# A hybrid decoder trunk in exact-split fp32r: one in-place weight sum per early seven-product group becomes an accumulating load

## The chip, the cores and the metric

The kernel runs on one core of one Trainium2 chip. The metric is device time in microseconds (us) of one execution. A core has a matrix engine (PE, with its weight loads as PEld), a vector engine (DVE), a scalar engine (ACT), a general engine (POOL, GpSimd), and SP, which here only issues transfers. Each engine runs its own instructions strictly in order; engines wait for one another and for transfers by semaphores. Transfers are issued from SP's queue, and some from POOL's.

## The reference, cut to what matters

One decoder layer takes 528 prompt tokens (16 of them meta tokens) and 8 sample tokens, width 2048:

```
h = rmsnorm(x) @ w_in                       # 2048 x 8704: q, k, v, z_a, u, z_s, g_a, g_s
o = sliding-window attention with sinks(q, k, v)
y = S5 state-space branch(u)                # diagonal complex recurrence per group
br_a = (o * silu(z_a)) @ w_attn_out ; br_s = (y * silu(z_s)) @ w_ssm_out
out = x + (sigmoid(g_a) * br_a + sigmoid(g_s) * br_s) @ w_out
```

The result is wanted in fp32. Nearly all the time goes to the products with the weights.

## The kernel before, in words

**Split products.** A weight unit is 128 partitions x 1024 fp32 elements (512 KB). For use it is split in two: ACT casts it to a high part `whi` (L1074), DVE makes the low part `wlo = raw - whi` (L1075), and PE forms high times high, high times low and low times high for each of eight 128x128 pieces, 24 matmuls of 260 columns per product of a seven-product group.

**Seven products in place of eight.** The class `Quads` (L1026 to L1086) serves places where a 2x2 block product is made with seven products (Strassen's way) in place of eight. A group has four units, loaded as `raw[0]` to `raw[3]`, and seven products, numbered here 0 to 6 in the order in which `make` splits their weights. Product 0 uses unit 0 and product 1 unit 1. Before product 2 DVE adds unit 2 into unit 1, in place; before product 3 it adds unit 0 into unit 1 (tuple `(1, 0)` in `SUMS`) and unit 0 into unit 2 (tuple `(2, 0)`); before product 4 it adds unit 3 into unit 1. Product 5 uses unit 3, and product 6 uses unit 2 as summed. So the sum (2, 0) is wanted by product 6 only. These sums are L1073.

There are 15 **early groups** (two column blocks of `w_in` each; `self.fourth` is None there) and, at the kernel's end, 8 **late groups** for `w_out`. In the first late group (`r < 7 and self.fourth`) the sum (2, 0) is already made without DVE: POOL issues a second load of unit 0 whose transfer adds into `raw[2]` (L1070). In all others DVE makes it.

**Order.** Loads, casts, sums and splits are written some three products ahead of the matmuls and carry high priority. A scheduler then sets, before the program runs, the order of the instructions on each engine. The accumulator banks of PE are emptied by ACT (`keep3`, L1394; L1416) and DVE (L1422, L1417, L1432, then the evacuation L1200). In an early group PE's order is: product 0, then product 6 of the group before in the midst of it, 1, 2, 3, a few matmuls of 5, then 4, then the rest of 5. Product 4 adds into the bank that product 2 filled, and so may start only when ACT's L1394 has emptied that bank.

**Work beside it.** During the early groups POOL computes the constants of the state-space branch (`ssm_prep`, L149 to L299, on `OnPool`): some 200 small instructions, one chain, each waiting for one before it, tile `work`. Its result is stored by L1499 (`kept`) and transposed by PE (L291) later.

Of the kernel before, what the change touches and what calls it, by code (L numbers as in the profile page):

```python
# [12 lines left out]
ALU = mybir.AluOpType  # L13
# [976 lines left out]
class Stream:  # L990
# [20 lines left out]
    def make(self, i):  # L1011
        with self.tc.high_priority(offset=HIGH):
            self.piece(i, self.tiles(i), slice(0, 8))
# [12 lines left out]
class Quads:  # L1026
# [29 lines left out]
    def make(self, r):  # L1056
        nc = self.nc
        q, s = divmod(r, 7)
        if self.LOADS[s] is not None:
            self.load(4 * q + self.LOADS[s] + 4)  # L1060
        if r < 7 and self.fourth:
            s = (0, 1, 2, 5, 3, 4, 6)[s]
        t = self.raw[4 * q + self.SRC[s]]
        pool, bufs = (self.pool, 3) if r % (3 + self.mp) < 3 else (self.more, self.mp)
        hi = pool.tile([P, 8, P], F32R, name="whi", bufs=bufs)
        lo = pool.tile([P, 8, P], F32R, name="wlo", bufs=bufs)
        with self.tc.high_priority(offset=HIGH):
            for oi in self.SUMS[s]:
                if r < 7 and self.fourth and oi == (2, 0):
                    nc.gpsimd.dma_start(out=self.raw[2], in_=self.w[self.first], accum_op=ALU.add)  # L1070
                    continue
                o, i = (self.raw[4 * q + j] for j in oi)
                nc.vector.tensor_tensor(out=o, in0=o, in1=i, op=ALU.add)  # L1073
            nc.scalar.copy(out=hi, in_=t)  # L1074
            nc.vector.tensor_tensor(out=lo, in0=t, in1=hi.bitcast(F32), op=ALU.subtract)  # L1075
        self.parts[r] = hi, lo
# [873 lines left out]
```

## Time and profile before

| | |
|---|---|
| three runs, median | 1264.08 us (1263.49 to 1266.17) |
| span of the profiled execution | 1262.3 us; the page gives no other time for it. The median run is 1.8 us above this span |
| PE busy | 1250.9 us, 99% |
| DVE busy / ACT / POOL | 980.6 / 628.7 / 266.1 us |
| early groups | from about 112 to 420 us of the span |
| POOL's constants | from 112.8 to 266 us |
| late groups | from about 1096 us to the end |

Times in rows of the profile are microseconds from the span's start; a mean or a minimum of one instruction is in ns where the view says so. A row of the time line has start, duration, engine, line, operation, tiles and, in brackets, the idle time ahead and what ended it; "x3" merges three like instructions that follow each other. A row of the busy time by stretch has the length of the stretch, then busy time and number of instructions of PE, PEld, DVE, ACT and POOL, the granted clock of PE, the share of the transfer engines and GB/s. A busy PE means back-to-back matmuls, about 0.12 us apart.

### The profile page before, as it was taken

To read this page: it belongs to the slowest core of one execution; us is meant where nothing else is said; L and a number is where in the kernel's file an instruction comes from. 1 tells how busy PE (TensorE), PEld (TensorE's weight loads), DVE (VectorE), ACT (ScalarE), POOL (GpSimd) and SP (SyncE) were. 2 spreads that over 40 slices of the span, in tenths; PEclk is the share of its full clock that TensorE was granted. 3 is DMA by queue.
4 is the path that set the end of the run, shared out by engine and by line. 5 is a ranking of instruction groups with operands and counts; after the bars stand their busy time and mean duration, and the time that the engine had idled before them with its cause. 6 is when DMAs were issued, how large, how long until landed. Compare 5 with 4: busy or idle time off the path is not lost.

```text
span 1262.3 us, 26537 instructions
## 1 busy us (share of the span) xinstructions
PE 1250.9 (99%) x10357; PEld 1227.7 (97%) x10357; DVE 980.6 (78%) x1554; ACT 628.7 (50%) x1344; POOL 266.1 (21%) x437
## 2 busy tenths in 40 slices
PE   9999999999999999999999999999999999999998
PEld 9999999999999999999999999999999999999998
DVE  8687878887778668888897377899887577887875
ACT  8554445444545586556432235567555333344342
POOL 0003999940000033122220123211011000000000
PEclk9999999999999999999999989999999999999999
DMA  8544343443434656555554775777666756555441
GB/s 294 199 160 153 134 143 110 143 150 134 151 126 146 214 172 182 159 165 167 156 159 121 246 211 182 224 240 225 189 214 203 258 174 189 165 192 163 145 139 51
DMA packets 108001, 219.22 MB, mean 174 GB/s; under 512 B 21932, under 2 KB 47492, under 8 KB 107844
## 3 DMA queue, kind: packets, MB, share of 16 engines
q1 hardware_dynamic: 99172, 198.53, 48.5%
q0 software_dynamic: 8704, 19.00, 5.6%
q8 instruction: 81, 1.33, 0.4%
q14 instruction: 44, 0.36, 0.1%
HBM read 181.57 MB, written 36.82 MB: 173 GB/s over the span
## 4 chain that ended last, share of the span: by engine, by line
PE 92%; DVE 3%; DMA 2%; ACT 1%; SPq 1%; issue 0%; DVEq 0%; ACTq 0%
PE mm L1168 45%; PE pr L1382 35%; PE wg L854 2%; PE mm L1255 2%; PE aux L1382 1%; PE aux L1168 1%; PE aux L1255 1%; DVE wlo L1009 1%; PE aux L806 1%; PE aux L805 1%; ACT ct L346 1%; PE tr L526 1%; PE tr L836 1%; PE wg L526 1%; DMA Y<-yD 0%
## 5 line engine op out<-in xcount | busy, mean ns | idle before, releaser
L1075 DVE TENSOR_TENSOR wlo<-raw,whi 128x1024 fp32r<-128x1024 f32 x161 | 198.5, 1253 | 69.6 <-ACT whi L1074 69.0
L1074 ACT CAST whi<-raw 128x1024 fp32r<-128x1024 f32 x161 | 166.4, 1049 | 167.2 <-DVE raw L1073 80.0
L1168 PE MATMUL mm<-xh,whi 128*128 128x260 f32 (+1 forms) x792 | 185.8, 288 | 3.1 <-DVE t L563 2.9
L1008 ACT CAST whi<-raw 128x1024 fp32r<-128x1024 f32 (+3 forms) x128 | 122.3, 965 | 132.3 <-PE mm L1168 85.6
L1168 PE MATMUL mm<-xh,wlo 128*128 128x260 f32 (+1 forms) x792 | 184.4, 287 | 0.0
L1168 PE MATMUL mm<-xl,whi 128*128 128x260 f32 (+1 forms) x792 | 184.1, 286 | 0.0
L1009 DVE TENSOR_TENSOR wlo<-raw,whi 128x1024 fp32r<-128x1024 f32 (+3 forms) x128 | 142.2, 1119 | 46.5 <-ACT whi L1008 45.7
L1382 PE MATMUL pr<-tau,whi 128*128 128x260 f32 x928 | 168.6, 283 | 0.0
L1382 PE MATMUL pr<-cb,whi 128*128 128x260 f32 x848 | 153.0, 283 | 0.0
L1382 PEld LDWEIGHTS pr<-tau,whi 128*128 128x128 f32 x928 | 143.0, 188 | 0.0
L1168 PEld LDWEIGHTS mm<-xh,whi 128*128 128x128 f32 x792 | 132.5, 189 | 5.8 <-ACT KH L747 3.1
L1168 PEld LDWEIGHTS mm<-xl,whi 128*128 128x128 f32 x792 | 133.1, 190 | 0.4 <-issue 0.4
L1168 PEld LDWEIGHTS mm<-xh,wlo 128*128 128x128 f32 x792 | 132.2, 189 | 0.4 <-issue 0.4
L1382 PEld LDWEIGHTS pr<-cb,whi 128*128 128x128 f32 x848 | 130.8, 188 | 0.2 <-ACT z L1416 0.2
L1382 PE MATMUL pr<-tau,wlo 128*128 128x260 f32 x464 | 130.8, 282 | 0.0
L1382 PE MATMUL pr<-cb,wlo 128*128 128x260 f32 x424 | 119.1, 283 | 0.2 <-DVE wlo L1075 0.2
L1073 DVE TENSOR_TENSOR raw<-raw 128x1024 f32<-128x1024 f32 x91 | 113.9, 1252 | 1.6
L1168 PE MATMUL mm<-Y,whi 128*128 128x260 f32 x576 | 105.1, 287 | 0.0
L1382 PE MATMUL pr<-xl,whi 128*128 128x260 f32 x352 | 98.9, 283 | 0.0
L1382 PE MATMUL pr<-xh,wlo 128*128 128x260 f32 x352 | 98.8, 283 | 0.0
L1382 PE MATMUL pr<-xh,whi 128*128 128x260 f32 x352 | 97.1, 283 | 0.0
L1382 PEld LDWEIGHTS pr<-tau,wlo 128*128 128x128 f32 x464 | 87.2, 188 | 0.0
(421 smaller groups left out, 2974.9 us busy)
## 6 DMA issues: line engine op xcount, KB each, us to landing
raw<-in_w SPq DMA_DIRECT2D x202, 512.0 KB, 4.3
gD<-z SPq DMA_DIRECT2D x34, 260.0 KB, 4.3
t<-gD SPq DMA_DIRECT2D x32, 260.0 KB, 3.1
cache<-in_vc POOLq DMA_DIRECT2D x16, 286.0 KB, 3.5
cache<-in_kc POOLq DMA_DIRECT2D x15, 288.0 KB, 4.0
xr<-in_x SPq DMA_DIRECT2D x16, 268.0 KB, 6.5
xg<-in_x SPq DMA_DIRECT2D x8, 536.0 KB, 4.7
sbw<-rawD SPq DMA_DIRECT2D x16, 260.0 KB, 5.1
```

The lines of the kernel that those rows point to most:

```text
L346: nc.scalar.activation(out=dst, in_=src, func=AF.Copy, scale=x)
L526: nc.tensor.matmul(o[n], lhsT=D["CL"][:, 2 * e + n, i, 1:5], rhs=H[:, 2 * e + n, i, 0:140], start=False, stop=(i == 1))
L805: nc.tensor.matmul(ps[:, e, 0:272], lhsT=q, rhs=KH[:, k0:k0 + 272], start=True, stop=False)
L854: nc.tensor.matmul(pv[64 * e:64 * e + 64, 0:256], lhsT=V, rhs=pr[:, e::2], start=(i == 0), stop=(i == len(parts) - 1))
L1008: nc.scalar.copy(out=hi, in_=raw)
L1009: self.dve = nc.vector.tensor_tensor(out=lo, in0=raw, in1=hi.bitcast(F32), op=ALU.subtract).ins
L1073: nc.vector.tensor_tensor(out=o, in0=o, in1=i, op=ALU.add)
L1074: nc.scalar.copy(out=hi, in_=t)
L1075: nc.vector.tensor_tensor(out=lo, in0=t, in1=hi.bitcast(F32), op=ALU.subtract)
L1168: m = nc.tensor.matmul(ps[:, c, 0:W], lhsT=wt[:, k], rhs=xo(kt, c), start=f, stop=l)
L1255: nc.tensor.matmul(ps[:, c, 0:260], lhsT=wt[:, kt % 8], rhs=xk(xo, kt, c, 8), start=f, stop=l)
L1382: m = nc.tensor.matmul(bank, lhsT=wt[:, p], rhs=x(p, e), start=first and f and p == 0, stop=l and p == 7, skip_group_check=not first and l ...
```

## The change

The condition for the accumulating load is widened from the first late group to the early groups, and the indices are made general:

```
             for oi in self.SUMS[s]:
-                if r < 7 and self.fourth and oi == (2, 0):
-                    nc.gpsimd.dma_start(out=self.raw[2], in_=self.w[self.first], accum_op=ALU.add)
+                if oi == (2, 0) and (r < 7 or not self.fourth):
+                    nc.gpsimd.dma_start(out=self.raw[4 * q + 2], in_=self.w[self.first + 4 * q], accum_op=ALU.add)
                     continue
```

The late groups stay as they were: the first has its accumulating load, the other seven their DVE sum. In each of the 15 early groups one DVE sum of 128x1024 goes, and POOL issues one more transfer of 512 KB from DRAM that adds into unit 2. It can be issued once unit 2 has been added into unit 1, since that sum reads unit 2.

On DVE, in the second early group and the start of the third (`raw_1696` and `raw_1819` are units 1 and 2 of the third group, `raw_1541` is unit 2 of the second, and the last brackets name the semaphores waited for, DMASW those of transfers issued by POOL):

```order
 L1075 TENSOR_TENSOR wlo_1822<-raw_1499,whi_1821 128x1024 [waits Activation_49]
 L1075 TENSOR_TENSOR wlo_1851<-raw_1630,whi_1850 128x1024 [waits Activation_49]
-L1075 TENSOR_TENSOR wlo_1881<-raw_1541,whi_1880 128x1024 [waits PE_49,Activation_49]
+L1075 TENSOR_TENSOR wlo_1881<-raw_1541,whi_1880 128x1024 [waits DMASW1_49,PE_49,Activation_49]
 L1075 TENSOR_TENSOR wlo_1911<-raw_1662,whi_1910 128x1024 [waits DMAHW0_49,PE_49,Activation_49]
 L1075 TENSOR_TENSOR wlo_1943<-raw_1696,whi_1942 128x1024 [waits DMAHW7_49,PE_49,Activation_49]
 L1073 TENSOR_TENSOR raw_1696<-raw_1696,raw_1819 128x1024 [waits DMAHW1_49,DVE_49]
-L1073 TENSOR_TENSOR raw_1819<-raw_1819,raw_1662 128x1024 [waits DVE_49]
 L1075 TENSOR_TENSOR wlo_1977<-raw_1696,whi_1976 128x1024 [waits PE_49,Activation_49]
```

The sum is gone, and the split of product 6 of the second group (`wlo_1881`) now waits for a transfer of POOL's queue; its place is the same.

On ACT, at the same place (`t_1732<-pr2_1734` is an L1394 emptying a bank; `whi_1821`, `whi_1850` and `whi_1880` are the casts of products 4, 5 and 6 of the second group):

```order
 L1074 CAST whi_1821<-raw_1499 128x1024 [waits DVE_49]
 L1074 CAST whi_1850<-raw_1630 128x1024 [waits DMAHW6_49,PE_49]
-L1074 CAST whi_1880<-raw_1541 128x1024 [waits PE_49,Activation_49]
+L1074 CAST whi_1880<-raw_1541 128x1024 [waits DMASW1_49,PE_49,Activation_49]
 L1394 ACTIVATE t_1732<-pr2_1734 128x260 [waits PE_49]
 L1202 ACTIVATE z_1493<-z_1493 128x520 [waits DVE_49]
```

The order of ACT in the early groups is otherwise that of before: the cast of product 6 gets a wait more, and behind it stand, in every group, the L1394s that empty the second and third banks.

On POOL, at the second of the new transfers (the rows around it are `ssm_prep`'s; L42 and L43 are its multiply-add):

```order
 L42 TENSOR_SCALAR work<-work 128x64
 L43 TENSOR_TENSOR work<-work 128x32
+L1070 DMA raw<-in_w 128x1024
 L43 TENSOR_TENSOR work<-work 128x64
 L60 TENSOR_SCALAR work<-work 128x32
```

and at the end of that chain (L283 is its last instruction):

```order
 L283 TENSOR_TENSOR work<-work 128x64
 L1499 DMA kept<-work 128x1920
+L1070 DMA raw<-in_w 128x1024 x11
 L1567 MEMSET T 32x4x32
 L1567 MEMSET T 64x4x64
```

The first transfer stands ahead of the chain's first instruction; the second behind 50 rows of the program on POOL, the third 59 rows later, right behind L228; the fourth 60 rows later, right behind an L243; the fifth 38 rows after that, behind L1499, with the other ten following it directly.

## The prediction

> **What bounds the kernel now.** I read the page's head first, then the list of what PE waited for, then the busy time by stretch around the early groups, and last the time lines of POOL, DVE, ACT and PE there.
>
> ```profile
> span 1262.3 us, 26537 instructions
> ## 1 busy us (share of the span) xinstructions
> PE 1250.9 (99%) x10357; PEld 1227.7 (97%) x10357; DVE 980.6 (78%) x1554; ACT 628.7 (50%) x1344; POOL 266.1 (21%) x437
> ...
> L1073 DVE TENSOR_TENSOR raw<-raw 128x1024 f32<-128x1024 f32 x91 | 113.9, 1252 | 1.6
> ```
>
> PE is the bound; a change can gain only what PE stands idle, 11.4 us in all, and loses whatever it makes PE wait. The busy time by stretch, for the early groups while POOL computes its constants and after:
>
> ```profile
> 112.00:266.00 154.00, 154.00 (x1284) 154.00 (x1283) 129.43 (x124) 73.71 (x101) 146.37 (x206) 1.00 0.38 127
> 266.00:420.00 154.00, 154.00 (x1284) 154.00 (x1283) 117.70 (x126) 72.75 (x104) 0.63 (x1) 1.00 0.43 146
> ```
>
> PE has no idle time at all in 308 us. DVE has some 60 us to spare. POOL is 95% busy until 266 (146.37 of 154) and then free. So the 15 sums that leave DVE, 15 x 1.25 = 18.8 us, are off the path: their removal is worth 0 here, since the matmuls hide them, and it would cost 0 to put them back.
>
> **What the new transfer costs by itself.** The one of its kind in this trace, in the first late group, with its time from issue to landing, and the ordinary load of a unit:
>
> ```profile
> L1070 POOL DMA_DIRECT2D raw<-in_w x1: 961/961/961, 1096.1 to 1096.1; - x1
> ...
> DMA to landing us min/median/max: 8.2/8.2/8.2
> ```
> ```profile
> raw<-in_w SPq DMA_DIRECT2D x202, 512.0 KB, 4.3
> ```
>
> I take 8.2 us, from the same operation, and 4.3 as the lower end. 15 x 512 KB, 7.9 MB, join transfer engines that are at a share of 0.38 to 0.43 there, so bandwidth hides them; were it short, SP's loads would land later, and they have a group's lead. The Trainium skill ("DMA: Bandwidth & Descriptors", Anatomy of one DMA, SWDGE path) gives about 2.0 us plus bytes / 436e3 for such a transfer, an estimate of 3.2 us here. No run here shows so little for this transfer, and by it the sum below would be about 5 us smaller.
>
> In groups 6 to 15 POOL is free and the load is issued when units 1 and 2 are summed. For the sixth group:
>
> ```profile
> 208.20 2.61 DVE L1073 TENSOR_TENSOR raw<-raw 128x1024 f32<-128x1024 f32 x2
> ```
> ```profile
> 220.12 1.05 ACT L1074 CAST whi<-raw 128x1024 fp32r<-128x1024 f32 x1
> ```
>
> The first of the two sums ends at 209.5, the cast of product 6 starts at 220.1; 10.6 us hold the 8.2. These ten cost 0, and so does the first group's, whose issue is ahead of POOL's chain.
>
> **Where it costs: POOL's queue.** The transfers of groups 2 to 5 stand inside POOL's chain, behind L43, L228, L243 and L1499. When POOL passed these places:
>
> ```profile
> 147.65 2.50 POOL L43 TENSOR_TENSOR work<-work 128x32 f32<-128x32 f32 x2
> ...
> 186.46 0.38 POOL L228 TENSOR_SCALAR work<-work 128x64 f32<-128x64 f32 x1
> ...
> 227.19 1.99 POOL L243 TENSOR_TENSOR work<-work 128x384 f32<-128x384 f32 x1
> ...
> 265.84 0.80 POOL L1499 DMA_DIRECT2D kept<-work  x1 [0.32 <-POOL work L283]
> ```
>
> That is 148.9 (between the two L43), 186.8, 229.2 and 266.6: some 40 us apart. The groups come 20 us apart. PE's first matmul of product 4 in groups 2 and 5 (the second of each row; four groups, so 19.9 us each):
>
> ```profile
> 146.47 0.40 PE L1382 MATMUL pr<-xh,whi 128*128 128x260 f32 x2
> ...
> 206.28 0.40 PE L1382 MATMUL pr<-xh,whi 128*128 128x260 f32 x2
> ```
>
> So product 4 is due at 146.6, 166.5, 186.4 and 206.4. What it waits for on ACT, in group 2:
>
> ```profile
> 138.40 2.95 ACT L1074 CAST whi<-raw 128x1024 fp32r<-128x1024 f32 x3 [2.02 <-DVE raw L1073]
> ...
> 143.24 0.38 ACT L1394 ACTIVATE t<-pr 128x260 f32<-128x260 f32 x1
> ```
>
> The third cast, at 140.3, is product 6's; it would wait for the landing. Behind it in ACT's order are the casts of the next group and the L1394 that empties product 4's bank, done 3.3 us after that cast's start. So PE waits for landing + 3.3 us at product 4, though product 6 itself comes later. DVE stops too, at the split of product 6, the third of these rows in groups 2 and 5:
>
> ```profile
> 140.53 4.70 DVE L1075 TENSOR_TENSOR wlo<-raw,whi 128x1024 fp32r<-128x1024 f32 x4
> ...
> 199.05 3.77 DVE L1075 TENSOR_TENSOR wlo<-raw,whi 128x1024 fp32r<-128x1024 f32 x3
> ```
>
> at 142.9 and 201.6 (19.6 us apart), and goes on 1.2 us after the landing. That matters because POOL runs faster while DVE stands:
>
> ```profile
> 126.06 0.25 POOL L62 TENSOR_TENSOR work<-work 128x32 f32<-128x32 f32 x1
> 126.40 0.30 POOL L63 TENSOR_SCALAR work<-work 128x32 f32<-128x32 f32 x1
> 126.79 1.23 POOL L62 TENSOR_TENSOR work<-work 128x32 f32<-128x32 f32 x1
> ...
> 205.28 0.25 POOL L77 TENSOR_TENSOR work<-work 128x32 f32<-128x32 f32 x1
> 205.49 0.25 POOL L78 TENSOR_TENSOR work<-work 128x32 f32<-128x32 f32 x1
> ```
>
> The same L62 took 0.25 and 1.23 us. The quick ones follow at 0.21 to 0.34 us, against 37.9 / 59 = 0.64 and 42.4 / 60 = 0.71 us over the stretches between the places. I take a factor of 2 while DVE stands, since some instructions are wide, and 1 and 3 for the ends. The Trainium skill ("SBUF — State Buffer", Who interferes with whom) says that a DVE instruction with two SBUF inputs and a GpSimd instruction that reads SBUF exclude each other, the second waiting until the first is done. By that rule POOL is freed outright while DVE stands, nearer the factor 3 and a sum of +26; the two times of L62 agree with the rule in kind, but no row here shows DVE standing for 10 us.
>
> **The sum, group by group.** "POOL time" is time of the trace's own pace.
> - Group 2: at DVE's stop, 142.9, POOL has 6.0 to go, 3.0 at double pace; issue at 145.9, landing 154.1, L1394 done 157.4, due 146.6: PE is 10.8 us late. DVE goes on at 155.3.
> - Group 3: from 146.9 to 155.3 POOL does 16.8 of its 37.9. DVE's stop is at 162.4 + 10.8 = 173.2, until when POOL does 17.9 more; the last 3.2 take 1.6. Issue 174.8, landing 183.0, L1394 186.3, due 166.5: late by 19.8.
> - Group 4: 16.8 of 42.4 by 184.2; stop at 201.8, 17.6 more; 8.0 left take 4.0. Issue 205.8, landing 214.0, 217.3 against 186.4: late by 30.9.
> - Group 5: 16.8 of 37.4 by 215.2; stop at 232.5, 17.3 more; 3.3 left take 1.7. Issue 234.2, landing 242.4, 245.7 against 206.4: late by 39.3.
>
> Nothing gives this back: PE is full. A wait of PE has one price more. In this trace the longest wait of PE ended just before 742, and PE ran slower after it:
>
> ```profile
> PE mm L1168 <- DVE t L563: 2.9, 1, 2.9
> ```
> ```profile
> 742.00:750.00 8.00, 8.00 (x48) 8.00 (x48) 7.36 (x21) 1.32 (x3) 2.74 (x6) 0.66 1.09 263
> ```
>
> A granted clock of 0.66 over 8 us is 2.7 us lost. After the first three waits the next wait, which ends by POOL's clock, swallows that; after the last it adds 2.7. Sum: 39.3 + 2.7 - 0 = +42.0; span 1304.3, and with the 1.8 us of the median run above the span 1306.1 us. POOL's own delay by four issues (4 x 0.96) is in the chain and delays nothing else, as its results are wanted by PE only at 330, 64 us later:
>
> ```profile
> L291 PE MATMUL tr<-k_idn,work x2: 271/272/272, 330.5 to 330.6; 128*128 128x128 f32 x2
> ```
>
> The ends: landing in 4.3 leaves the issue times almost where they are and takes 3.9 off, 1302. Factor 3 gives issues at 144.9, 167.0, 196.7 and 218.3, late by 23.4 at the last, +26, 1290. Factor 1 is a rival.
>
> **The rivals.**
> - POOL does not speed up (factor 1). The fifth transfer is issued at 266.6 plus three earlier issues, 269.5; 269.5 + 8.2 + 3.3 - 206.4 = 74.6, with the clock 77.3: 1341. For it: POOL's chain has semaphore waits between most instructions, and L243 and its like are long anyway. Against: the two times of L62.
> - The loads come in time after all, and nothing changes: 1264. It needs an issue by 146.6 - 11.5 = 135.1 in group 2, when POOL would have to be 13.8 us ahead of the trace, and worse later. For it: DVE has one sum less per group. Against: that frees 1.25 of 20 us only, and POOL's queue is strict.
> - Faster: the only wait of some size that DVE causes is that at L563, 2.9 us and 2.7 of slow clock. Would relieved DVE or an earlier end of POOL's chain remove it, 1258.5. The point from which it decides: all loads in time, and 18.8 us of DVE carried over 320 us of a full PE. Against: POOL and DVE both have slack between 266 and 742, so nothing is carried that far.
>
> **How the numbers follow.** Late loads with a partly freed POOL: 0.74, own range 1285 to 1320. No speed-up: 0.13, 1341. In time: 0.08. Faster: 0.05. A measurement of this kernel tells about 0.2%, 2.5 us, from no change. So slower 0.87, same 0.08, faster 0.05. The range runs from under the factor 3 to the rival with factor 1, 1284 to 1341.
>
> **What would show it.** Right: PE idle at L1382 in four places between 140 and 250 us, each 8 to 12 us, ended by ACT's L1394, and ACT's L1074 waiting for the transfer `raw<-in_w` of POOL in the same four; POOL's instructions shorter there, L1499 at some 233 in place of 266; the granted clock below 1 after each; from group 6 on PE full; L1073 x76. Wrong: POOL passes L43 before 136, landing times far above 8.2 (then more groups stall), or PE idle in groups 6 to 15.

## The result and the profile after

The changed kernel takes 1295.5 us (median of 4 runs, 1294.3 to 1301.9) against 1265.1 us for the kernel before (4 runs): the ratio is 1.0253, with a 95% interval of 1.0228 to 1.0279. It is slower by about 30 us. The forecast was 1306, with a range of 1284 to 1341. The profiled execution has a span of 1293.5 us, 31.2 more than before.

The page of the changed kernel, head and busy times, and the row of DVE's sums:

```profile
span 1293.5 us, 26573 instructions
...
PE 1257.6 (97%) x10357; PEld 1233.4 (95%) x10357; DVE 963.9 (75%) x1539; ACT 627.7 (49%) x1344; POOL 231.5 (18%) x452
...
L1073 DVE TENSOR_TENSOR raw<-raw 128x1024 f32<-128x1024 f32 x76 | 93.0, 1223 | 1.1
```

The 15 sums are gone (76 in place of 91, DVE 16.7 us less), and POOL's work has become shorter by 34.6 us without one instruction of its chain removed. Where PE now stands is in its list of waits (what waited, for whom, us in all, times, longest), and beside it the line of ACT's list that is new:

```profile
PE pr L1382 <- ACT t L1394: 14.7, 2, 7.6
PE pr L1382 <- ACT z L1394: 6.9, 1, 6.9
PE mm L1168 <- DVE t L563: 3.1, 1, 3.1
PE pr L1382 <- DVE wlo L1075: 1.4, 2, 1.2
PE pr L1382 <- DVE t L1417: 1.4, 1, 1.4
```
```profile
ACT whi L1074 <- DMA raw<-in_w: 31.8, 3, 11.3
```

Three waits of PE at product 4, of 7.1, 6.9 and 7.6 us, each ended by ACT's L1394, and three waits of ACT's cast for the transfer. With the two small waits for DVE that follow the third, PE stands 24.1 us in the early groups. Before, it stood 0 there. The busy time by stretch (us, PE, PEld, DVE, ACT, POOL, granted clock, transfer share, GB/s):

```profile
112.00:266.00 154.00, 129.89 (x1013) 128.84 (x1012) 98.10 (x92) 56.74 (x78) 104.86 (x213) 0.92 0.46 131
266.00:420.00 154.00, 154.00 (x1283) 154.00 (x1283) 111.54 (x115) 73.38 (x102) 5.96 (x7) 1.00 0.56 161
```

All of it lies before 266 us, and the granted clock is below 1 there. After 266 PE is full as before. After its waits PE ran at half speed for 4.7, 3.4, 4.5 and 3.3 us, which loses 8.0; with the 24.1 us of standing that is 32.1, within 1 us of the 31.2 by which the span grew.

The transfer's own view (the row of its issues, and the last line of the view):

```profile
L1070 POOL DMA_DIRECT2D raw<-in_w x16: 811/857/996, 111.8 to 1127.4; - x16
...
DMA to landing us min/median/max: 5.2/5.4/8.4
```

Group 2 shows the whole mechanism in ACT's time line; the first matmul behind it on PE is the second fence:

```profile
150.64 1.04 ACT L1074 CAST whi<-raw 128x1024 fp32r<-128x1024 f32 x1 [10.34 <-DMA raw<-in_w]
151.59 0.38 ACT L1394 ACTIVATE t<-pr 128x260 f32<-128x260 f32 x1
...
152.39 1.03 ACT L1074 CAST whi<-raw 128x1024 fp32r<-128x1024 f32 x1
153.33 0.39 ACT L1394 ACTIVATE t<-pr 128x260 f32<-128x260 f32 x1
```
```profile
153.77 0.59 PE L1382 MATMUL pr<-xh,whi 128*128 128x260 f32 x1 [7.06 <-ACT t L1394]
```

The load was issued at 145.1 and landed at 150.5. The cast of product 6 runs at 150.6, behind it come an L1394, a cast of the next group and the second L1394, done at 153.7, and then PE's product 4 starts, 7.1 us late.

### The profile page after: what moved, and what is told of

It reads as the page before. It is cut to its first block, busy times and chain, and to the rows that moved or that the text cites. A ratio compares the mean times of both kernels' runs of the same rounds, so it can differ in the third digit from the quotient of the medians.

```text
span 1293.5 us, 26573 instructions
## 1 busy us (share of the span) xinstructions
PE 1257.6 (97%) x10357; PEld 1233.4 (95%) x10357; DVE 963.9 (75%) x1539; ACT 627.7 (49%) x1344; POOL 231.5 (18%) x452
## 4 chain that ended last, share of the span: by engine, by line
PE 81%; DMA 4%; DVE 4%; POOL 4%; ACT 2%; issue 2%; SPq 1%; DVEq 0%; ACTq 0%; POOLq 0%
PE mm L1168 43%; PE pr L1382 30%; PE wg L854 2%; DMA xr<-in_x 1%; PE aux L1168 1%; DVE wlo L1009 1%; DMA raw<-in_w 1%; DVE wlo L1075 1%; PE aux L806 1%; PE aux L805 1%; PE mm L1693 1%; ACT ct L346 1%; PE tr L836 1%; POOL work L62 1%; PE tr L526 1%
## 5 line engine op out<-in xcount | busy, mean ns | idle before, releaser
L1075 DVE TENSOR_TENSOR wlo<-raw,whi 128x1024 fp32r<-128x1024 f32 x161 | 203.4, 1279 | 115.6 <-ACT whi L1074 113.3
L1382 PE MATMUL pr<-tau,whi 128*128 128x260 f32 x928 | 170.3, 285 | 1.4 <-DVE t L1417 1.4
L1382 PE MATMUL pr<-cb,whi 128*128 128x260 f32 x848 | 153.0, 283 | 0.0
L1382 PEld LDWEIGHTS pr<-tau,whi 128*128 128x128 f32 x928 | 144.5, 190 | 1.6 <-DVE t L1417 1.6
L1382 PE MATMUL pr<-tau,wlo 128*128 128x260 f32 x464 | 131.7, 284 | 0.0
L1382 PEld LDWEIGHTS pr<-cb,whi 128*128 128x128 f32 x848 | 130.9, 189 | 0.2 <-ACT z L1416 0.2
L1382 PE MATMUL pr<-xh,whi 128*128 128x260 f32 x352 | 100.8, 292 | 21.5 <-ACT t L1394 14.7
L1382 PE MATMUL pr<-cb,wlo 128*128 128x260 f32 x424 | 119.1, 283 | 0.2 <-DVE wlo L1075 0.2
L1382 PE MATMUL pr<-xh,wlo 128*128 128x260 f32 x352 | 101.5, 290 | 1.2 <-DVE wlo L1075 1.2
L1382 PE MATMUL pr<-xl,whi 128*128 128x260 f32 x352 | 101.4, 290 | 0.0
L1073 DVE TENSOR_TENSOR raw<-raw 128x1024 f32<-128x1024 f32 x76 | 93.0, 1223 | 1.1
L1382 PEld LDWEIGHTS pr<-xh,whi 128*128 128x128 f32 x352 | 68.4, 197 | 22.1 <-ACT t L1394 15.1
```

The lines of the kernel that those rows point to most:

```text
L1382: m = nc.tensor.matmul(bank, lhsT=wt[:, p], rhs=x(p, e), start=first and f and p == 0, stop=l and p == 7, skip_group_check=not first and l ...
```

## The experiments

In the diffs, `q` counts the early groups from 0, so `q == 1` is group 2. Where an edit adds lines, the lines behind it have higher numbers: L1385, L1392 and L1393 are the matmuls of L1382, L1397, L1404 and L1405 the L1394, and L1080 is the L1070. In the second run on ACT's order L1075 is the cast, L1076 the split and L1422 the L1417; in the last run L1086 is the split.

**Which loads cost: group 2 alone, group 5 alone, groups 1 to 5, groups 6 to 15.** The condition for a load is the same line each time:

```diff
-                if oi == (2, 0) and (r < 7 or not self.fourth):
+                if oi == (2, 0) and (r < 7 if self.fourth else q == 1):   # group 2 alone
+                if oi == (2, 0) and (r < 7 if self.fourth else q == 4):   # group 5 alone
+                if oi == (2, 0) and (r < 7 if self.fourth else q < 5):    # groups 1 to 5
+                if oi == (2, 0) and (r < 7 if self.fourth else q >= 5):   # groups 6 to 15
```

Group 2 alone:

> Only group 2 loads into unit 2; in POOL's order the load stands three rows further on than in the changed kernel. My theory: one idle time of PE at L1382 of 7 to 9 us that starts at 146.6, then a granted clock of 0.5 for 6.8 us, in which PE loses another 3.4 us: 1275.5 to 1278 in all, if the slow clock is to be paid in full where no further wait follows. Rival, the slow clock is not lost because PE has been short of something else: 1272 to 1274. Rival, 2 us for each load: 1267.

Measured 1278.3 us, ratio 1.0104 (1.0068 to 1.0139), at the upper end of what was expected. PE stands once, for 10.1 us and not 7 to 9, and the clock stays at 0.5 after it, for 4.8 us and not 6.8:

```profile
PE pr L1382 <- ACT t L1394: 10.1, 1, 10.1
```
```profile
157.20:162.00 4.80, 4.72 (x22) 4.72 (x22) 4.68 (x4) 0.97 (x2) 4.72 (x5) 0.50 0.81 248
```

4.8 us at half speed are 2.4 us lost, so 12.5 us are accounted for, of the 14.1 by which this execution (1279.4 us) lies above the kernel before (1265.3). The load was issued at 148.3, three rows of POOL later than in the changed kernel (145.1), and that is the difference of its wait from 7.1.

Group 5 alone:

> Only group 5 loads into unit 2, one load in place of fifteen; in POOL's order it stands behind L1499, the end of the chain, which was at 266.6 us before. My theory: the place in POOL's queue makes the price, so this one load costs as much as all fifteen. DVE stops at 201.6 and POOL then has 65 us of its old pace to go. At double pace: issue 234, landing 239.5, L1394 done 242.8, due 206.4, PE idle once for some 36 us, and about 3 us of slow clock: 1304. At three times the pace: issue 223, idle 26 us, 1294. At the old pace: issue 267, idle 69 us, 1337. So 1290 to 1305 with one idle time of PE of 25 to 36 us. Rival, a price for each load: 2 us, 1267. Rival, one wait costs what one wait of the changed kernel costs (7 us and its slow clock): 1275.

Measured 1300.8 us, ratio 1.0282 (1.0261 to 1.0303). One load costs as much as all fifteen, or a little more. The 33.0 us of its one wait and 1.8 us of slow clock behind it make 34.8 of the 35.5. The waits of PE, and POOL's time line at the end of its chain:

```profile
PE pr L1382 <- ACT z L1394: 33.0, 1, 33.0
```
```profile
228.98 0.80 POOL L1499 DMA_DIRECT2D kept<-work  x1 [0.32 <-POOL work L283]
229.82 0.91 POOL L1070 DMA_DIRECT2D raw<-in_w  x1
```

The place in POOL's queue sets the price, not the number of loads. DVE stood from 201.5 on; POOL needed 27.5 us from there to L1499, for what took 64.3 us of the trace before (201.5 to 265.8). That is a factor of 2.3 while DVE stands. PE and ACT stand then too, so this run alone doesn't say that DVE is the one that matters. The records of the kernel before do: there PE never stands in this stretch, and all 87 instructions of POOL's chain that took over 0.9 us ran beside one of DVE, while the 51 that had none of DVE beside them took at most 0.57 us.

Groups 1 to 5:

> Only groups 1 to 5 load into unit 2; groups 6 to 15 keep DVE's second sum. My theory: these five carry the whole change, 1295.5 within 2.5 us, with the same three idle times of PE of 7 us at L1382. Rival, 2 us for each load: 5 x 2 = 10 us, 1275.

Measured 1299.1 us (1296.2 to 1301.7), ratio 1.0267 (1.0238 to 1.0297), whose interval overlaps the changed kernel's; the time is 1 us above the expected band. The five early loads carry the whole change, with waits of 7.5, 7.2 and 6.3 us at L1394.

Groups 6 to 15:

> Only groups 6 to 15 load into unit 2; groups 1 to 5 keep DVE's second sum. My theory: a load costs nothing where POOL's queue is empty, since its issue follows the sum at once and its 5.4 us to landing lie in a lead of some 10 us, so the time is that of before, 1265, within 2.5 us, with PE full from 112 to 420 us. Rival, each load costs by itself (its 512 KB, DVE or ACT held while it is under way): 30.4 us / 15 = 2 us each, ten of them 20 us, 1285. Rival, relieved DVE is worth something at the wait at L563 further on: 1258 to 1262.

Measured 1290.3 us, ratio 1.0197 (1.0174 to 1.0221). My expectation missed by 25 us. The waits of PE and POOL's time line:

```profile
PE pr L1382 <- ACT t L1394: 24.4, 1, 24.4
```
```profile
240.11 0.80 POOL L1499 DMA_DIRECT2D kept<-work  x1 [0.31 <-POOL work L283]
240.94 0.91 POOL L1070 DMA_DIRECT2D raw<-in_w  x1
254.97 0.87 POOL L1070 DMA_DIRECT2D raw<-in_w  x1 [13.12 <-DVE raw L1073]
```

The load of group 6 is issued behind L1499 at 240.9, and PE's product 4 was due at 226.6. In the changed kernel group 6 is free only because the earlier waits have stopped DVE and brought POOL to the end of its chain at 224; without them the chain is still running when group 6 comes. It is the same mechanism one group later. From group 7 on POOL waits for DVE's sum (13.12 us idle before the issue) and PE has no wait. POOL's factor while DVE stood was again 2.4 (18.8 us, from 221.3 to 240.1, for 44.5).

**Loads with POOL's queue empty.** The right control is then the groups that come after the chain at its old pace:

```diff
+                if oi == (2, 0) and (r < 7 if self.fourth else q >= 9):   # groups 10 to 15
```

> Only groups 10 to 15 load into unit 2; they are the first whose load is wanted after POOL's chain has ended at its old pace (266.6; the load of group 10 can be issued at some 290). The run with groups 6 to 15 had its load of group 6 behind that chain. My theory: where POOL has nothing ahead of the load, it costs nothing: 1265 within 2.5 us, no idle time of PE at L1382 between 110 and 420, no slow clock there. Rival, a price of the load itself, 2 us each: six of them, 1277. Rival, relieved DVE is worth something: 1258 to 1262.

Measured 1265.2 us, ratio 1.0011 (1.0001 to 1.0022). That is 0.1%, and at the interval's upper end 0.2%, some 0.5 us for each of six loads. PE is full in both stretches:

```profile
112.00:266.00 154.00, 154.00 (x1283) 154.00 (x1282) 129.42 (x124) 73.74 (x101) 146.46 (x206) 1.00 0.39 128
266.00:420.00 154.00, 154.00 (x1284) 154.00 (x1283) 111.09 (x121) 72.55 (x104) 5.70 (x7) 1.00 0.56 166
```

**What the relief of DVE is worth.** The sum is left out and no load put in its place:

```diff
+                if oi == (2, 0) and not self.fourth:
+                    continue
```

> The fifteen early groups leave out the sum of unit 0 into unit 2, by DVE and by load (product 6 uses unit 2 alone there). It shows what the relief of DVE, 15 x 1.25 = 18.8 us, is worth with nothing in its place. My theory: 0, since the matmuls cover it: 1265 within 2.5 us. Rival, relieved DVE gains at the wait at L563 (2.9 us and its slow clock): 1258.5. Rival, DVE keeps PE waiting in ways that the trace doesn't name: down to 1247.

Measured 1264.7 us, ratio 1.0004 (0.9989 to 1.0018). The 18.8 us of DVE work are worth nothing.

**ACT's order, first attempt.** The cast of product 6 is written later and ordered behind an L1394:

```diff
-            nc.scalar.copy(out=hi, in_=t)
+            with self.tc.issue_after(self.kept) if s == 6 and not self.fourth else ExitStack():
+                nc.scalar.copy(out=hi, in_=t)
...
+            if not self.fourth and self.made % 7 == 6 and self.made > self.i + 1:
+                break
...
-                nc.scalar.activation(out=kept[n][0], in_=first[n][0], func=AF.Copy, scale=kept[n][1])
+                qs.kept = nc.scalar.activation(out=kept[n][0], in_=first[n][0], func=AF.Copy, scale=kept[n][1]).ins
```

> The changed kernel, but on ACT the cast of product 6 in the early groups stands behind the L1394 that empties the bank of product 2 and so lets product 4 start; POOL's order is as in the changed kernel. My theory: PE no longer waits at product 4, but only for the casts of the next group, which still stand behind that cast and are wanted some 6 us later. With landings 5.4 us after issue and POOL 2.36 times as fast while DVE stands (44.5 us of its old pace took 18.8 us in the run with groups 6 to 15, 65 took 27.5 us in the run with group 5 alone): issues at 145, 169, 193 and 216, PE late by 1, 4, 8 and 13 us, so 1275 to 1283. Rival, PE lacks product 6 itself, and ACT's order doesn't matter: 1295. Rival, the later cast makes PE wait in every early group: over 1300.

Measured 1298.1 us, ratio 1.0268 (1.0250 to 1.0287); PE has waits of 8.3, 6.2 and 7.2 us. The edit missed its aim: `kept` held the last L1394 written, that of product 1's bank, which ACT empties first. The L1394 of product 2's bank stayed behind the cast, and so did PE. It says nothing against or for the theory, except that product 1's bank is not what product 4 lacks.

**ACT's order, second attempt.** `kept` is set where `n == 2`, which is product 2's bank:

```diff
-                qs.kept = nc.scalar.activation(out=kept[n][0], in_=first[n][0], func=AF.Copy, scale=kept[n][1]).ins
+                m = nc.scalar.activation(out=kept[n][0], in_=first[n][0], func=AF.Copy, scale=kept[n][1]).ins
+                if n == 2:
+                    qs.kept = m
```

> As the run before that moved ACT's cast of product 6, but now it stands behind the L1394 of product 2's bank; there it stood only behind that of product 1's bank, which is emptied first, and the three idle times of PE were left as they were. My theory: PE waits at product 4 for the emptying of product 2's bank and for nothing else, so the waits there go; what is left are waits for the casts of the next group, some 6 us later, by my sum 1, 4, 8 and 13 us late after groups 2 to 5: 1275 to 1283. Rival, PE lacks product 6 itself or the next group's weights just as soon: 1295 to 1299.

Measured 1298.6 us, ratio 1.0258 (1.0236 to 1.0280). No gain. The waits of PE (L1422 adds a bank to a result on DVE):

```profile
PE pr L1385 <- DVE t L1422: 14.3, 2, 13.0
PE pr L1385 <- ACT whi L1075: 7.2, 2, 3.8
PE pr L1385 <- DVE wlo L1076: 1.8, 3, 0.8
PE pr L1385 <- DVE z L1422: 1.3, 1, 1.3
```

Half of my theory holds: the waits for L1394 are gone altogether, so they were made by ACT's order. The other half fell: PE waits just as long a few us later, 24.6 us in these rows against 24.4 in those of the changed kernel at L1382. ACT's next casts (L1075) and DVE's next splits and sums all stand behind the late load, so the first two groups lost 5.8 and 5.5 us instead of 1 and 3. Most of the third loss, 13.0 us at 212 to 225, came from DVE:

```profile
213.32 10.35 DVE L1076 TENSOR_TENSOR wlo<-raw,whi 128x1024 fp32r<-128x1024 f32 x2 [8.76 <-ACT whi L1075]
223.71 1.22 DVE L1073 TENSOR_TENSOR raw<-raw 128x1024 f32<-128x1024 f32 x1
224.86 0.41 DVE L1422 TENSOR_TENSOR t<-t,pr 128x260 f32<-128x260 f32 x1
```

Two splits that take some 1.2 us each elsewhere took 10.35 us together, some 8 us too long, while POOL ran its chain to its end (last section).

**All fifteen loads, with POOL's chain behind them.** Each instruction of the chain after the first 18 is ordered, on POOL alone, behind the last load written before it, and the chain's budget per product is 0.3 in place of 0.4:

```diff
-GBUDGET = 0.4
+GBUDGET = 0.3
+HOLD, FREE = [None, 0], 18
 class OnPool:
...
-        return getattr(self.e, name)
+        f = getattr(self.e, name)
+        def held(*a, **k):
+            HOLD[1] += 1
+            with HOLD[0]() if HOLD[0] and HOLD[1] > FREE else ExitStack():
+                return f(*a, **k)
+        return held
...
-                    nc.gpsimd.dma_start(out=self.raw[4 * q + 2], in_=self.w[self.first + 4 * q], accum_op=ALU.add)
+                    self.sent = nc.gpsimd.dma_start(out=self.raw[4 * q + 2], in_=self.w[self.first + 4 * q], accum_op=ALU.add).ins
...
+            HOLD[0] = (lambda: tc.issue_after(qs.sent)) if q < NQ - 1 else None
             bg.step(GBUDGET if q < NQ - 1 else 1.2)
+            HOLD[0] = None
```

> All fifteen loads as in the changed kernel, but POOL's chain of constants is ordered behind them in pieces: its first 18 instructions before the load of group 2, and each later one behind the last load written before it (order on POOL alone, no work removed; the chain's budget per product is 0.3 in place of 0.4, so its pieces are written over some twelve groups). By POOL's old pace of 0.64 to 0.71 us an instruction the load of group 3, with about 36 instructions ahead of it, would be issued at 153 to 157 and must be by 157.8; the later ones have as many or fewer. My theory: the loads come in time, PE has no idle time over 3 us at L1382 before 420, and the time is that of before, 1265, within 4 us. Rival, the loads cost by themselves (2 us each, or held up by each other): 1285 to 1295. Rival, the later chain now keeps PE waiting at L291 or the kept constants come late: 1270 to 1290, with idle time of PE after 320.

Measured 1272.0 us, ratio 1.0067 (1.0050 to 1.0083): three quarters of the loss gone, but above my band by 3 us. One wait is left in the early groups, and POOL's time line shows why:

```profile
PE pr L1392 <- ACT t L1404: 6.1, 1, 6.1
```
```profile
157.70 0.92 POOL L1080 DMA_DIRECT2D raw<-in_w  x1
...
183.62 0.92 POOL L1080 DMA_DIRECT2D raw<-in_w  x1 [0.24 <-issue]
```

Group 3's load was issued at 157.7, just ahead of the 157.8 it needed. Then 35 instructions took 25 us, and group 4's, at 183.6, was 6 us late: I had counted groups of 35 instructions as if 20 us held them.

**The same with that piece cut in two.** One piece of the chain ends earlier, so that 12 instructions stand between the loads of groups 3 and 4, and 23, 26 and 28 before the next:

```diff
+    yield 1.5
     v.tensor_tensor(out=s, in0=r, in1=r, op=ALU.mult)
...
-    yield 3.0
+    yield 2.0
```

> As the run that spread POOL's chain behind the loads, with one piece of the chain cut in two (budgets of 1.5 and 2.0), so that 12 instructions in place of 35 stand between the loads of groups 3 and 4, and 23, 26 and 28 before the next ones. There 35 instructions took 25 to 26 us and made the load of group 4 issue at 183.6, some 6 us too late; that was its only wait. My theory: now each load's issue is ahead of its due time, PE has no idle time over 1 us at L1382 from 110 to 420, and the time is that of before, 1265, within 2.5 us, with all fifteen loads. Rival, something else of the loads or of the later chain costs the 7 us: 1270 to 1274.

Measured 1265.6 us (1262.1 to 1268.8), ratio 1.0006 (0.9995 to 1.0016). All fifteen loads are there, and the time is that of before. PE in the early groups, and the waits at L1382 that are left in the whole kernel:

```profile
112.00:266.00 154.00, 153.83 (x1280) 153.62 (x1279) 116.97 (x116) 73.51 (x101) 108.13 (x162) 1.00 0.55 157
266.00:420.00 154.00, 154.00 (x1283) 154.00 (x1283) 115.34 (x119) 72.78 (x104) 45.14 (x59) 1.00 0.57 167
```
```profile
PE pr L1393 <- DVE wlo L1086: 0.2, 1, 0.2
PE pr L1393 <- ACT z L1405: 0.2, 1, 0.2
```

It has the same 15 transfers and the same chain of POOL in another order: 108.1 us of POOL's work before 266 and 45.1 after it. The chain now ends at 363 us in place of 266, and PE's two transposes of its result (L291), at 330.5 before, stand at 393.7; PE stands nowhere for them. So the 30 us are neither bandwidth nor the transfer's own cost, but the place of the first few in POOL's queue. It is no gain over the kernel before: DVE's relief is worth nothing here either.

## Why the prediction was right, and where its sizes were off

**DVE's relief worth 0: shown.** Leaving the sum out altogether gave 1.0004.

**Groups 6 to 15 and group 1 cost 0: right for this kernel, for a reason that the text only half gave.** POOL was called free from group 6 on. It was, but only because the waits of groups 2 to 4 had brought the end of its chain forward from 266 to 224; with the early loads taken away, group 6 alone cost 24.4 us of PE.

**The loads stand in POOL's chain, and that sets the end: shown** by the load of group 5 alone (+36 us for one load) and by the reordered chain (+1 us for fifteen).

**ACT's order brings the wait to product 4: shown as far as the place goes.** With the cast moved the waits at product 4 vanish. That it makes the loss larger, as "though product 6 itself comes later" suggests, is not shown: PE lost as much without it.

**Issue times.** The forecast had 145.9, 174.8, 205.8 and 234.2; the trace has 145.1, 174.0, 204.0 and 224.2. Three are within 1.8 us. Of the four waits of 8 to 12 us that were to show it, three came, of 6.9 to 7.6 us, and L1499 stands at 223.6, not at 233. The step that failed is the last one, group 5. The forecast gave POOL its double pace only while DVE stands and the old pace from then on, 28.4 us from the fourth load to the fifth; it took 20.2. DVE was ready to go on at 210.6 but got nowhere for 6 us: one split took 7.2 us in place of 1.2, with POOL's chain beside it, and POOL ran on at its quick pace almost to the end of the chain (rows in the last section). So the fifth load landed at 231.8 and its L1394 came in time: three big waits, not four, and 2.6 us of small waits for DVE in place of the 8.4 us more that group 5 was to cost.

**Landing.** The forecast took 8.2 us, "from the same operation". Measured: 5.5, 5.4, 5.2 and 5.4 us for groups 1 to 4 and a median of 5.4, against 7.6 for group 5, right behind L1499's transfer, and 8.4 for the late group. The one row of before stood in a crowded stretch (a transfer share of 0.87 from 1096 to 1105, against 0.38 in the early groups before 266) and wasn't typical; no run separates the crowding from other causes. The Trainium skill ("DMA: Bandwidth & Descriptors", Anatomy of one DMA) gave an estimate of 3.2 us; the measured 5.4 lies between the two.

**The clock.** The forecast let the next wait swallow the slow clock of all waits but the last, and after the first that is how it went: 7.2 us late after group 2's wait, PE would have come to group 3's product 4 at 173.3 (166.1 + 7.2) and came at 175.6, 2.3 us of slow clock later; its wait ended with ACT's L1394 all the same.

The sum: the forecast had PE 30.9 us late after group 4, the trace 25.9 (212.1 against the due 186.2 of the trace before, which the forecast put at 186.4). Of these 5.0, 2.8 are the landing and 1.8 the fourth issue. Group 5 and the clock were to add 8.4 + 2.7 = 11.1, and added 5.3 (31.2 - 25.9). Together 10.8 of +42.0; 31.2 is left.

**The chances.** The factor for POOL, taken as 2 between 1 and 3, came out as 2.3 to 2.4 where DVE stood for long. "No speed-up", 1341, is out by these rows. "In time" is what the reordered chain shows: it needed another order, not a faster POOL. "Faster" is out too: the wait at L563 is still there (3.1 us), and without the sum and without a load the time stayed (1.0004).

## What to carry to other kernels

A transfer that is issued by an engine with work of its own can come as late as what stands ahead of it in that engine's queue; look up its row in the order and the time at which the engine passed that row before, and compare with the due time. An engine that seems free from some point on may be free only because of the waits that the change makes, so a part of a change can cost as much as the whole. Where the work ahead isn't urgent (here POOL's constants, whose use at 330.5 us could move to 393.7), ordering it behind the transfers removed the cost without removing any work; but taking work off DVE, which wasn't waited for, gained nothing.

## What the runs showed of the hardware that was not expected

**POOL can keep DVE out over many instructions.** The time of DVE's split (min/median/max in ns), over the whole trace of before and then over that of the changed kernel:

```profile
L1075 DVE TENSOR_TENSOR wlo<-raw,whi x161: 1215/1226/2147, 102.9 to 1246.0; 128x1024 fp32r<-128x1024 f32 x161
```
```profile
L1075 DVE TENSOR_TENSOR wlo<-raw,whi x161: 1160/1226/7234, 102.9 to 1277.2; 128x1024 fp32r<-128x1024 f32 x161
```

The 7.23 us are one split that began at 210.6; in the second run on ACT's order one took 9.2. The changed kernel's time lines of DVE and POOL there:

```profile
210.62 10.08 DVE L1075 TENSOR_TENSOR wlo<-raw,whi 128x1024 fp32r<-128x1024 f32 x2 [10.71 <-ACT whi L1074]
```
```profile
210.28 0.40 POOL L76 TENSOR_TENSOR work<-work 128x64 f32<-128x64 f32 x1
210.55 0.65 POOL L75 TENSOR_TENSOR work<-work 128x192 f32<-128x192 f32 x1
211.09 0.64 POOL L76 TENSOR_TENSOR work<-work 128x192 f32<-128x192 f32 x1
...
216.64 1.32 POOL L241 TENSOR_TENSOR work<-work 128x32 f32<-128x32 f32 x1
```

POOL's instructions are quick (0.25 us for 128x32) and each begins before the one ahead has ended, until at 216.6 one of 128x32 takes 1.32 us; then DVE's split ends, at 217.9. So the two engines hold each other up in turns, and a string of POOL's can hold DVE for 6 us. The long wait ahead of the split isn't the reason. After the wait of the run with group 5's load alone POOL has nothing to do, and three splits take 3.67 us together:

```profile
238.45 3.67 DVE L1075 TENSOR_TENSOR wlo<-raw,whi 128x1024 fp32r<-128x1024 f32 x3 [36.95 <-ACT whi L1074]
```

And in no run did one of these splits that had no instruction of POOL beside it take over 1.23 us. The Trainium skill ("SBUF — State Buffer", SBUF: two separate sides) says of the port pair that DVE and GpSimd share that whichever of their instructions starts first has the pair for its whole length and the other blocks fully. Both directions agree with these rows; that the loser was held over sixteen instructions of POOL, and over nineteen for the 9.2 us, and not over one goes beyond the sentence.

**The clock falls during the wait and lasts after it.** After the changed kernel's three waits of 7 us the granted clock was 0.5 for 3.4 to 4.7 us of work, after that of 24.4 us (groups 6 to 15) for 6.0 us and after that of 33 us (group 5 alone) for 3.6 us. The price is 1.7 to 3.0 us a wait, and it doesn't grow with the wait's length (1.8 us after the longest):

```profile
153.70:158.50 4.80, 4.73 (x22) 4.74 (x23) 3.43 (x3) 0.95 (x2) 4.56 (x8) 0.50 0.79 246
```
```profile
240.00:244.00 4.00, 4.00 (x20) 4.00 (x21) 3.93 (x4) 0.86 (x1) 0.00 (x0) 0.55 0.41 131
```

The first row is the changed kernel after its first wait, the second the run with group 5's load alone after its 33 us.
